# Row-wise argmax of an 8192 x 8192 matrix: loading row pairs as single 64 KB descriptors

## Chip, cores, metric

One core of one Trainium2 chip. The metric is the device time of one execution in microseconds (us), lower is better. Each kernel was executed several times, the kernel before always on the same chip in the same rounds. All runs quoted here are in the undisturbed (fast) state, with a granted TensorE clock of 1.0.

## The reference

```python
x = np.random.randn(8192, 8192).astype(np.float32)
def reference(x):
    return np.argmax(x, axis=1)
```

268 MB are read once; 8192 indices (64 KB) are written.

## The kernel before

The rows are worked on in 64 tiles of 128 rows (one row per partition, 32 KB). VectorE reduces a tile to the maxima of 128 chunks of 64 values (`cm`) and then to the row's maximum (`mx`). GpSimd copies the winning chunk of each row together (`ga`), ScalarE compares it with the maximum, TensorE sorts the matches into `sums`, and VectorE reads the place within the chunk out of them. The gathered copy is the last reader of a tile's 32 KB buffer, and it is put off (`defer`) until half of the next tile has been reduced, so that VectorE needn't wait for the small operations before it.

```python
xpool = ctx.enter_context(tc.tile_pool(name="x_sbuf", bufs=5))      # five buffers of 32 KB
# ...
def load_reduce(t, cm, loads, widths):
    xt = xpool.tile([P, M], F32, tag="xt")
    at = 0
    for w in loads:
        keep(nc.sync.dma_start(out=xt[:, at:at + w], in_=x[t * P:(t + 1) * P, at:at + w]))
        at += w
    at = 0
    for w in widths:
        # cm[:, chunks of this piece] = max over each chunk of 64
        keep(nc.vector.reduce_max(out=cm[:, c0:c1], in_=xt[:, at:at + w].rearrange(...), axis=AX.X))
        at += w
        step[0] = t * 8 + at // 1024
        run_due()                          # what was put off to this step
    return xt

def lookup(t, cm, xt, sums, k_after, last):
    # mx (VectorE), sc (ScalarE), wc (GpSimd) ...
    def copy_chunks():
        keep(nc.vector.reduce_max(out=k, in_=wc, axis=AX.X))
        # idx on GpSimd ...
        keep(nc.gpsimd.indirect_copy(ga, xt.rearrange("p (n h) -> p n h", h=H), idx, ...))   # frees xt
        # eq on ScalarE, 17 matmuls into sums ...
        if last:
            defer(12, lambda: finish(t - 3, 4, sums))
    defer(k_after, copy_chunks)

for t in range(63):
    # ...
    if t < 48:   loads, widths = [M], [M // 2] * 2        # whole tile in one transfer
    elif t < 60: loads = widths = [M // 2] * 2            # halves
    else:        loads = widths = [M // 4] * 4            # quarters
    xt = load_reduce(t, cm, loads, widths)
    lookup(t, cm, xt, sums, 4 if t < 60 else 2, t % 4 == 3)
# tile 63 has a direct way of its own ...
```

## Time and profile before

| | before |
|---|---|
| time, median | 642.61 us (642.29 to 643.03, 3 runs) |
| profiled span | 640.7 us |
| VectorE (DVE) busy | 596.8 us, 93% |
| DMA queue of x | 97.9% of 16 engines, 419 GB/s over the span |
| GpSimd, ScalarE, TensorE busy | 25%, 15%, 12% |

How to read it: the transfers of x are issued by SyncE (SP) on one queue, which 16 DMA engines work off. A buffer's next load can be issued when its last reader is done. As long as the queue never runs empty, the DMA engines set the pace; VectorE has about 0.4 us per tile to spare. The prediction below shows the lines.

### The profile page before, as it was taken

What the parts mean: (1) busy time and instruction counts of PE and PEld (TensorE: products, weight loads), DVE (VectorE), ACT (ScalarE), POOL (GpSimd) and SP (SyncE); (2) the same over time, 40 slices, a digit from 0 to 9 for tenths busy, and PEclk for the clock granted to TensorE, in tenths of its full rate; (3) what the DMA queues carried; (4) which work ended last, traced back from release to release, by engine and by line L of the source; (5) the groups of instructions that cost most, each with busy time, mean ns of one, the idle gap of its engine ahead of it and who ended that gap; (6) DMA issues with size and microseconds to landing.
All of it is one profiled execution on the core that took longest, in us unless ns stands there. A gap on an engine that the chain in (4) does not pass through costs nothing.

```text
span 640.7 us, 3237 instructions
## 1 busy us (share of the span) xinstructions
PE 77.0 (12%) x1079; PEld 66.7 (10%) x1079; DVE 596.8 (93%) x293; ACT 93.1 (15%) x130; POOL 160.0 (25%) x210
## 2 busy tenths in 40 slices
PE   0011010110110110110111101101101111110111
PEld 0011010110110110110110101101101110110110
DVE  1999989999999999999999999999999999999996
ACT  0011011011110110110110110111111110110121
POOL 4112212122122122222221221221221222222221
DMA  9999999999999999999999999999999999999991
GB/s 381 436 428 426 438 435 432 429 426 437 434 432 430 426 429 440 432 432 427 428 438 432 428 433 430 434 432 429 434 419 429 428 428 428 429 430 420 421 419 69
DMA packets 13233, 268.74 MB, mean 419 GB/s; under 512 B 1618, under 2 KB 1681, under 8 KB 2209
## 3 DMA queue, kind: packets, MB, share of 16 engines
q1 hardware_dynamic: 13104, 268.44, 97.9%
q8 instruction: 8, 0.13, 0.1%
q10 hardware_dynamic: 81, 0.06, 0.0%
q0 software_dynamic: 32, 0.03, 0.0%
q14 instruction: 8, 0.07, 0.0%
HBM read 268.47 MB, written 0.07 MB: 419 GB/s over the span
## 4 chain that ended last, share of the span: by engine, by line
issue 54%; POOL 21%; ACT 9%; DVE 8%; DMA 7%; POOLq 0%; PE 0%; ACTq 0%; SPq 0%; DVEq 0%
POOL ga L158 14%; DMA xt<-in_x_dram 7%; DVE cm L122 7%; ACT eq L160 5%; POOL wc L148 4%; ACT sc L147 3%; POOL idx L154 3%; DVE zi L221 0%; DVE z L217 0%; POOLq L158 0%; DVE k_all L152 0%; DVE mx L143 0%; PE ps L133 0%; ACTq L138 0%; DVE k_all L175 0%
## 5 line engine op out<-in xcount | busy, mean ns | idle before, releaser
L122 DVE TENSOR_REDUCE cm<-xt 128x64 f32<-128x4096 f32 (+2 forms) x137 | 564.4, 4126 | 33.4 <-DMA xt<-in_x_dram 32.3
L160 ACT ACTIVATE eq<-ga,mx 128x1024 bf16<-128x1024 f32 x63 | 72.3, 1148 | 512.6 <-POOL ga L158 512.6
L158 POOL INDIRECT_COPY ga<-xt,idx 128x1024 f32 x63 | 104.3, 1656 | 134.3 <-issue 130.0
L165 PEld LDWEIGHTS <-sel_flat 128*128 128x128 bf16 x1008 | 59.8, 127 | 546.4 <-issue 543.5
L165 PE MATMUL sums<-eq,sel_flat 128*128 128x64 bf16 x1008 | 63.8, 239 | 431.4 <-ACT eq L160 431.4
L154 POOL TENSOR_SCALAR idx<-starts,k_all 128x2 uint16<-128x2 f32 x63 | 19.2, 304 | 218.7 <-DVE k_all L152 217.2
L148 POOL TENSOR_TENSOR wc<-descC,sc 128x128 f32<-128x128 f32 x63 | 28.8, 457 | 117.0 <-ACT sc L147 117.0
L163 PE MATMUL sums<-descL,ones 1*128 1x64 bf16 x63 | 13.9, 224 | 117.8 <-DVE k_all L175 111.2
L147 ACT ACTIVATE sc<-cm,mx 128x128 f32<-128x128 f32 x63 | 24.4, 387 | 22.5 <-DVE mx L143 21.8
L143 DVE TENSOR_REDUCE mx<-cm 128x1 f32<-128x128 f32 x63 | 17.9, 284 | 4.8
L152 DVE TENSOR_REDUCE k_all<-wc 128x1 f32<-128x128 f32 x63 | 17.4, 276 | 0.4 <-POOL wc L148 0.4
L163 PEld LDWEIGHTS <-ones 1*128 1x128 bf16 x63 | 6.2, 98 | 12.0 <-POOL ones L87 6.4
L175 DVE TENSOR_REDUCE k_all<-sums 128x4 f32<-128x256 f32 (+1 forms) x16 | 6.6, 410 | 0.0
L132 PE MATMUL ps<-ident_m,k_all 128*60 128x128 f32 (+1 forms) x4 | 1.3, 420 | 5.9 <-DVE k_all L152 5.9
L188 POOL DMA_INDIRECT ga<-in_x_dram,idx x1 | 1.2, 1208 | 2.6 <-DVE idx L186 2.6
L81 POOL MEMSET sel_flat<- 128x2064 bf16 x1 | 1.8, 1818 | 0.0
L133 PE MATMUL ps<-ident,k_all 128*60 128x128 f32 (+1 forms) x4 | 1.3, 420 | 1.8 <-DVE k_all L175 1.8
L147 ACT ACT_TABLE_LOAD x1 | 1.3, 1283 | 0.7 <-PEq L252 0.7
L136 ACT ACTIVATE o<-ps 60x128 int32<-60x128 f32 (+1 forms) x2 | 0.6, 276 | 5.5 <-PE ps L133 5.5
L217 DVE MAX8 z<-xt 128x8 f32<-128x1024 f32 x1 | 1.2, 1221 | 0.0
L221 DVE FIND_INDEX8 zi<-z,xt 128x8 uint32<-128x1024 f32 x1 | 1.2, 1219 | 0.0
L82 POOL TENSOR_SCALAR sel_flat<-ident 128x128 bf16<-128x128 f32 x1 | 1.1, 1071 | 0.0
(32 smaller groups left out, 7.7 us busy)
## 6 DMA issues: line engine op xcount, KB each, us to landing
xt<-in_x_dram SPq DMA_DIRECT2D x48, 4096.0 KB, 29.9
xt<-in_x_dram SPq DMA_DIRECT2D x24, 2048.0 KB, 29.6
xt<-in_x_dram SPq DMA_DIRECT2D x14, 1024.0 KB, 21.1
xt<-in_x_dram SPq DMA_DIRECT2D x4, 512.0 KB, 14.5
out_dram<-o ACTq DMA_DIRECT2D x1, 60.0 KB, 6.1
ga<-in_x_dram,idx POOLq DMA_INDIRECT x1, 2.7
out_dram<-o ACTq DMA_DIRECT2D x1, 3.0 KB
out_dram<-o_last SPq DMA_DIRECT2D x1, 1.0 KB, 3.9
```

The lines of the kernel that those rows point to most:

```text
L81: nc.gpsimd.memset(sel_flat, 0.0)
L122: keep(nc.vector.reduce_max(out=cm[:, c0:c1], in_=xt[:, at:at + w].rearrange("p (c l) -> p c l", l=L), axis=AX.X))
L143: keep(nc.vector.reduce_max(out=mx, in_=cm, axis=AX.X))
L147: keep(nc.scalar.activation(out=sc, in_=cm, func=ACTF.Sign, bias=mx, scale=-1.0))
L148: keep(nc.gpsimd.tensor_tensor(out=wc, in0=descC, in1=sc, op=ALU.subtract))
L152: keep(nc.vector.reduce_max(out=k, in_=wc, axis=AX.X))
L154: keep(nc.gpsimd.tensor_scalar(out=idx, in0=starts, scalar1=k, scalar2=float(M), op0=ALU.subtract, op1=ALU.mult))
L158: keep(nc.gpsimd.indirect_copy(ga, xt.rearrange("p (n h) -> p n h", h=H), idx, i_know_this_is_slow=True))
L160: keep(nc.scalar.activation(out=eq, in_=ga, func=ACTF.Sign, bias=mx, scale=-1.0))
L163: nc.tensor.matmul(g, lhsT=ones, rhs=descL, start=True, stop=False)
L165: nc.tensor.matmul(g.rearrange("p (h l) -> p h l", h=2), lhsT=sel[:, r, :], rhs=eq.rearrange("p (h r) l -> p h r l", h=2)[:, :, r, :], sta ...
L175: keep(nc.vector.reduce_max(out=k2_all[:, t0:t0 + n], in_=sums[:, 0:n, :], axis=AX.X))
```

## The change

The intent: fewer and larger descriptors (a descriptor is one contiguous piece of a transfer, which the trace records as one packet). Rows 2p and 2p + 1 are neighbours in memory, so one descriptor of 64 KB brings both to partition p. Each five tiles come as pair, pair, single; a pair has a double buffer, so five buffers of 32 KB become two of 64 KB and one of 32 KB. Besides, tiles 48 to 53 come whole, the pieces of tiles 60 to 62 decrease, and the results of the paired rows have a store of their own.

```diff
-    xpool = ctx.enter_context(tc.tile_pool(name="x_sbuf", bufs=5))
+    xpool = ctx.enter_context(tc.tile_pool(name="x_sbuf", bufs=1))
 ...
-        xt = xpool.tile([P, M], F32, tag="xt")
+        if t % 5 in (0, 2):
+            xd = xpool.tile([P, 2, M], F32, tag="xd", bufs=2)
+            double[0] = xd
+            if t < PAIRED:                                     # PAIRED = 35
+                keep(nc.sync.dma_start(
+                    out=xd.rearrange("p j m -> p (j m)"),
+                    in_=x[t * P:(t + 2) * P, :].rearrange("(p j) m -> p (j m)", j=2)))
+        if t % 5 == 4:
+            xt = xpool.tile([P, M], F32, tag="xs", bufs=1)
+        else:
+            xt = double[0][:, (t % 5) % 2, :]
         at = 0
-        for w in loads:
+        for w in loads if t >= PAIRED or t % 5 == 4 else []:
 ...
-                defer(12, lambda: finish(t - 3, 4, sums))
+                defer(15, lambda: finish(t - 3, 4, sums))
 ...                          (store_paired: five small evictions and one store; cut)
-        if t < 48:
+        if t < 54:
             loads, widths = [M], [M // 2] * 2
 ...
-            loads = widths = [M // 4] * 4
+            loads = widths = [[4096, 2048, 2048], [3072, 3072, 2048], [3072, 2048, 2048, 1024]][t - 60]
```

Below, A and B are the two double buffers (tiles 0, 1 and 2, 3 of each five), S is the single one (tile 4).

More of the change, by code (lines that the diff above doesn't have):

```diff
@@ L35 @@
     NT = N // P
+    PAIRED = 35
     lpool = ctx.enter_context(tc.tile_pool(name="lead", bufs=1))
     gpool = ctx.enter_context(tc.tile_pool(name="gathered", bufs=2))
-    xpool = ctx.enter_context(tc.tile_pool(name="x_sbuf", bufs=5))
+    xpool = ctx.enter_context(tc.tile_pool(name="x_sbuf", bufs=1))
     epool = ctx.enter_context(tc.tile_pool(name="matches", bufs=2))
@@ L53 @@
     out_pairs = out_view([N, 2])
+    out_flat = out_view([2 * N])
     x_flat = x.tensor.reshape([N * C, L]).ap()
@@ L99 @@
     pending = []
+    double = [None]
     step = [0]
@@ L127, in load_reduce, with sum_parts, store_paired @@
         return xt
+    def sum_parts(ps, t0, n, step):
+        ts = slice(t0, t0 + (n - 1) * step + 1, step)
+        nc.tensor.matmul(ps, lhsT=k_all[:, ts], rhs=ident_m, start=True, stop=False)
+        nc.tensor.matmul(ps, lhsT=k2_all[:, ts], rhs=ident, start=False, stop=True)
+    def store_paired():
+        n = PAIRED // 5
+        o = opool.tile([n, 5 * P, 2], I32, tag="paired")
+        nc.gpsimd.memset(o, 0)
+        for u in range(5):
+            ps = ppool.tile([n, P], F32, tag="ps")
+            sum_parts(ps, u, n, 5)
+            if u < 4:
+                place = o[:, u // 2 * 2 * P:(u // 2 + 1) * 2 * P, 0].rearrange("c (p j) -> c p j", j=2)[:, :, u % 2]
+            else:
+                place = o[:, 4 * P:5 * P, 0]
+            keep(nc.scalar.activation(out=place, in_=ps, func=ACTF.Copy, scale=-1.0, bias=float(M + L)))
+        keep(nc.scalar.dma_start(out=out_flat[0:n * 10 * P].rearrange("(c q) -> c q", c=n),
+                                 in_=o.rearrange("c r two -> c (r two)")))
     def store(t0, n):
         ps = ppool.tile([n, P], F32, tag="ps")
-        nc.tensor.matmul(ps, lhsT=k_all[:, t0:t0 + n], rhs=ident_m, start=True, stop=False)
-        nc.tensor.matmul(ps, lhsT=k2_all[:, t0:t0 + n], rhs=ident, start=False, stop=True)
+        sum_parts(ps, t0, n, 1)
         o = opool.tile([n, P, 2], I32, tag=f"o{t0}")
@@ L175, in finish @@
         keep(nc.vector.reduce_max(out=k2_all[:, t0:t0 + n], in_=sums[:, 0:n, :], axis=AX.X))
+        if t0 == 4 * (PAIRED // 4):
+            store_paired()
         if t0 + n == 60:
-            store(0, 60)
+            store(PAIRED, 60 - PAIRED)
     def direct_begin(t, cm):
```

## The prediction

> **What bounds the kernel now.** I read the page first (engine shares, then the 40 slices), then the rates by stretch, then the waits, then the timeline of the first tiles, and last the chain of the final 90 us.
>
> ```profile
> DVE  1999989999999999999999999999999999999996
> DMA  9999999999999999999999999999999999999991
> L122 DVE TENSOR_REDUCE cm<-xt 128x64 f32<-128x4096 f32 (+2 forms) x137 | 564.4, 4126 | 33.4 <-DMA xt<-in_x_dram 32.3
> ```
>
> Two units look full. The DMA engines are busy in every slice but the last. VectorE is busy 93%, but the 33.4 us in which its reductions wait are nearly all put down to the load of x (13.1 us of them before the first tile). So the load of x sets the pace and VectorE follows closely: a tile costs DMA about 9.7 us and VectorE about 9.3 us (two reductions of 4.41 us, then mx and k_all, which add some 0.2 us each beyond overlap, and a quarter of the sums' 0.4 us).
>
> ```profile
> 100.00:200.00 100.00, 12.27 (x179) 10.90 (x179) 95.03 (x46) 15.85 (x22) 25.17 (x32) 1.00 1.00 430
> 480.00:590.00 110.00, 14.21 (x204) 12.58 (x204) 107.43 (x52) 17.29 (x24) 27.43 (x36) 1.00 1.01 427
> 592.00:612.00 20.00, 3.30 (x44) 2.65 (x44) 19.79 (x13) 4.03 (x5) 6.39 (x7) 1.00 1.01 421
> ```
>
> The last number of each line is GB/s, the one before it the DMA share. With descriptors of 32 KB (up to 479 us) it is about 431, with 16 KB 427, with 8 KB 421, always at full share. The engines never idle, so smaller descriptors cost time inside their own records. The packet records of the trace say how much: the median packet takes 161 ns at 4 KB, 312 at 8 KB, 614 at 16 KB and 1215 at 32 KB. Each doubling falls short of twice by 10, 10 and 13 ns, so a descriptor costs about 11 ns plus 36.7 ns per KB.
>
> ```profile
> 22.80 4.42 DVE L122 TENSOR_REDUCE cm<-xt 128x64 f32<-128x4096 f32 x1 [0.62 <-DMA xt<-in_x_dram]
> 27.14 0.28 DVE L152 TENSOR_REDUCE k_all<-wc 128x1 f32<-128x128 f32 x1
> 29.99 1.65 POOL L158 INDIRECT_COPY ga<-xt,idx 128x1024 f32 x1 [2.15 <-issue]
> 31.67 0.33 SPq L117 DMA_DIRECT2D xt<-in_x_dram  x1
> ```
>
> This is how a buffer comes free: tile 1 lands and its first half is reduced from 22.80; only then come tile 0's k, its index and its gathered copy; the copy ends at 31.64, and SP issues the load into tile 0's buffer at 31.67. That is **8.87 us from the landing of the next tile to the refill**. The refilled queue still holds 20 us of loads, so nothing is lost; the median of 29.9 us from issue to landing says the same (three tiles deep).
>
> ```profile
> 554.90 34.67 DMA xt<-in_x_dram
> 589.57 0.02 issue
> 589.60 4.43 DVE cm L122
> ```
>
> The chain leaves the load at 589.6 us; from there VectorE runs almost without a gap to the last result at 635.5. The end is the landing of tile 59's second half plus a fixed 46 us of VectorE and 5 us of final store.
>
> **What the Trainium skill says.** "DMA: Bandwidth & Descriptors", section "Where 436 GB/s comes from", puts the fabric ceiling at 435.2 GB/s; this trace, at 431, leaves under 1% to gain from any shape of descriptor. The same page under "Measured (HBM→SBUF, 128 partitions, SWDGE, issued from GpSimd)" gives about 10.5 ns per packet; my 11 ns from the packet records agrees, on loads issued from SP. Its section "Anatomy of one DMA — SWDGE (gpsimd) path" gives about 2.0 us of fixed cost per transfer, mostly completion. Here the first load is issued at 0.73 us and VectorE starts on it at 13.11: 12.4 us, of which 8 descriptors per engine are 9.7, so about 2.6 us on a cold queue. "VectorE: DVE Perf Modes", section "The perf-mode tier table (the rule you actually need)", has tensor_reduce at 1x only: 4096 values in 4414 ns agrees, and nothing in the change makes a reduction cheaper.
>
> **The change, part by part.**
> (a) 64 KB descriptors. Of 35 tiles, 28 go in 14 pairs. Each engine moves 8 descriptors per transfer, so 28 x 8 = 224 descriptors of 32 KB become 112 of 64 KB, if they are not cut up again. At 11 ns that saves 1.2 us. The 14 completions saved are about 9 ns each: 0.1 us. **Gain 1.3 us**, 0.2% of the span.
> (b) Tiles 48 to 53 in one transfer, not two: 6 x 8 descriptors fewer, **0.5 us**.
> (c) Tiles 60 to 62 have 10 pieces for 12: 16 descriptors fewer per engine, 0.2 us of DMA, and two reductions fewer. A reduction of 4096 takes 4414 ns and two of 2048 take 4552, so 0.14 us each: 0.3 us on VectorE's final run. The store of 60 rows, which now delays the 62nd tile's work (0.35 us wait of k_all on wc at 615.8), moves off. Together **0.6 us** on the path.
> (d) A pair lands as a whole and its buffer comes free as a whole. This is the cost. There are two double buffers (A, B) and a single one (S), filled A B S A B S. Pair A is free after its second tile's gathered copy, which happens in the middle of the first tile of B; that tile can start only when all of B has landed. So A's refill is issued 8.87 us after B's landing, and the only load left in the queue is S, which lands 9.72 us after B. Before, 20 us of loads were queued; now 0.85 us. A fresh transfer's first packet follows its issue by 1.0 us (first packet at 1.74 us in the trace, issue at 0.73), and data are gone from the queue some 0.34 us before the landing is seen. Bubble: 8.87 + 1.0 - (9.72 - 0.34) = **0.5 us at least**. To it comes what a dry queue pays at its start: the first packets of the run took 1.6 to 2.0 us, not 1.22, so 0.4 to 0.8 us. I take 0.35 to 0.65 of it, a bubble near 1.0 us. This happens at tiles 5, 10, 15, 20, 25, 30 and 35: **7 x 1.0 = 7 us**, between 3.4 and 10. B's refill is different: it is issued after tile 3's copy in the middle of tile 4, 18.6 + 8.87 = 27.5 us after B's landing, and A's data then last until about 29.7 us: just safe, by 1.2 us. S's refill is safe by 10 us. From tile 37 on, single loads land one by one and A's lead is 4 us and more again.
> (e) Something comes back: before, one of the 16 engines runs about 2.2 us behind the others by tile 16 (spread of the completion packets in the trace), and landings wait for it. In a bubble the others wait anyway and the lag goes away: **about 2 us** gained back.
> (f) VectorE starts at about 22.5 instead of 13.1 us. It waits for loads afterwards, so this is no loss by itself, but by tile 35 it is some 7 us behind the landings. At 9.72 - 9.28 = 0.44 us per tile it catches up in 16 tiles, by tile 51 to 55, before the tail at 59. Zero, but not by much. store_paired (five small evictions on ScalarE, one memset on GpSimd, a store) falls in an unpaired stretch on engines that are mostly idle: zero.
>
> Sum: 642.6 - 1.3 - 0.5 - 0.6 + 7 - 2 = 645.2; I shade it to **644.5**, since the cold-start term is the least certain one and a designer would hardly keep a change whose loss shows.
>
> **Rivals.** First, the gain with no bubble: if the refill reaches the queue in time (issue to first packet shorter than 1.0 us, or VectorE's half tile counted too long), it is 642.6 - 2.4 = 640.2. For it speaks that the margin in (d) is a few tenths; against it, that every term in (d) is read from this trace. Second, B's refills also come late: 1.2 us of margin is about one extra wait on GpSimd, and six or seven more bubbles make 649 to 652. Third, VectorE becomes the bound in the tail because it has not caught up: each tile missing costs 0.44 us, at most 2 to 3 us more. Fourth, 64 KB descriptors move data faster than the straight line says: the ceiling of 435 against 431 allows 1% of 273 us, 2.7 us, that is 638 at the very best with no bubble.
>
> **Range and chances.** The best combination is near 638, the central one 644.5, bubbles twice as costly 651. I take 640 to 649.5 for 8 in 10. A change of 2% needs 12.9 us either way: faster is beyond the fabric ceiling (1%), slower needs both A's and B's refills late and cold (3%).
>
> **What would show it.** Packets: 1792 data descriptors of 64 KB (14 x 128), some 2420 ns each, and 432 GB/s where the queue is full. Dips of the DMA share near 50, 100, 150, 200, 250, 300 and 350 us. VectorE's first reduction at about 22.5 us and its wait for x at some 45 to 50 us in all. In the timeline, the refill of A issued 8.9 us after the first reduction of a pair. Issue to landing of the pairs near 21 us for A. The tail chain from tile 59 to the end within 1 us of 51. I am wrong if the share shows no dips (then 640), if packets are still 32 KB (then only the bubbles remain), or if VectorE has no waits left in tiles 40 to 58 (then it has become the bound).

## The result and the profile after

| | before, same rounds | after |
|---|---|---|
| time, median of 5 runs | 642.29 us | 657.88 us (657.04 to 658.05) |
| ratio | | 1.0235, 95% interval 1.0221 to 1.0249 |

Ratios are the mean time of one kernel's fast runs over that of the other's of the same rounds, so not quite the ratio of the medians. The change is 2.3% slower, 15.6 us, and outside the predicted range.

From the page of the changed kernel: the busy tenths in 40 slices, and the group of the reductions (busy us, mean ns | idle before them and what ended it).

```profile
DVE  0699899899799899799799999999999999999997
DMA  9999999999999999998997999999999999999992
L137 DVE TENSOR_REDUCE cm<-xd 128x64 f32<-128x4096 f32 (+3 forms) x111 | 458.0, 4132 | 51.1 <-DMA xd<-in_x_dram 49.1
```

VectorE now shows an 8 or a 7 at every third slice (a slice is 16.4 us) through the first half of the run, and none after that until the last slice. It waits 49.1 us for x, not 32.3. The DMA row shows only two of the dips that were foreseen, as its 8 and its 7: an idle stretch of 1 to 2.5 us (below) is short beside a slice. The same stretch of five tiles in both kernels, in busy times by stretch (the last two numbers are the DMA share and GB/s); the first fence is the kernel after, from one landing of B to the next, the second the kernel before.

```profile
92.50:143.20 50.70, 5.88 (x89) 5.08 (x87) 46.17 (x21) 7.16 (x11) 12.04 (x15) 1.00 0.98 416
244.90:296.80 51.90, 6.03 (x86) 5.07 (x86) 46.50 (x22) 6.75 (x10) 12.05 (x15) 1.00 0.97 413
```

```profile
90.80:139.30 48.50, 5.90 (x85) 5.24 (x85) 45.44 (x20) 6.40 (x10) 11.57 (x15) 1.00 1.00 432
```

VectorE's work per five tiles is nearly the same (45.4 us before, 46.2 and 46.5 after); the cycle has become 2 to 3 us longer. (Each engine has its busy time and, in brackets, a count; VectorE's is the third pair.) Now the timeline of one refill of A in the changed kernel.

```profile
42.02 4.42 DVE L137 TENSOR_REDUCE cm<-xd 128x64 f32<-128x4096 f32 x1 [1.09 <-DMA xd<-in_x_dram]
46.35 0.28 DVE L186 TENSOR_REDUCE k_all<-wc 128x1 f32<-128x128 f32 x1
...
49.17 1.65 POOL L192 INDIRECT_COPY ga<-xd,idx 128x1024 f32 x1 [2.13 <-issue]
50.85 0.33 SPq L123 DMA_DIRECT2D xd<-in_x_dram  x1
...
72.72 4.42 DVE L137 TENSOR_REDUCE cm<-xd 128x64 f32<-128x4096 f32 x1 [2.97 <-DMA xd<-in_x_dram]
```

B lands and is started on at 42.02. Only after half of its first tile comes the gathered copy that frees A; the refill is issued at 50.85, **8.83 us** after the landing. It lands at 72.7, 21.9 us after its issue, while its eight descriptors per engine take 8 x 2.42 = 19.3 us. The remaining 2.5 us are the price of an empty queue. VectorE reaches the first tile of B at 42.02 and again, six rounds later, at 348.54: 51.1 us per five tiles, against 48.5 before. Tile 35 lands at 370.5 us and not at 354.5 (completions in the packet records plus the 0.34 us until VectorE sees them). So **16 us are lost in the first 35 tiles**, and the loss stays about the same to the end.

The packet records of the trace, which carry the start, length and size of every DMA packet, give the seven refills of A one by one. "Lead" is the mean time at which the 16 engines completed the previous transfer (each records a packet of 4 bytes then), less the issue of the refill. "Behind" is how much later the last engine completed B than the mean one. "Idle" is engine time with no packet, averaged over the 16 engines. "Slow" is what each engine's first two packets took beyond the usual 2418 ns each (1213 ns for tile 35's 32 KB), averaged in the same way.

| refill for tile | issued at | lead, us | B behind, us | idle, us | slow, us |
|---|---|---|---|---|---|
| 5 | 50.85 | 0.06 | 0.41 | 1.06 | 0.65 |
| 10 | 101.39 | -0.19 | 0.70 | 1.46 | 0.54 |
| 15 | 152.10 | -0.29 | 0.73 | 1.49 | 0.55 |
| 20 | 203.62 | -1.25 | 1.60 | 2.44 | 0.62 |
| 25 | 254.26 | -0.35 | 0.42 | 1.56 | 0.71 |
| 30 | 305.72 | -1.03 | 1.47 | 2.15 | 0.70 |
| 35 | 357.36 | -1.30 | 1.61 | 2.55 | 0.59 |
| sum | | | 6.9 | 12.7 | 4.4 |

Idle and slow add up to 17.1 us. There are 1792 packets of 64 KB with a median of 2418 ns, against two of 1213 ns: the fewer descriptors save 112 x 8 ns, 0.9 us. The balance, 16.2 us, agrees with the measured 16.0.

The end of the chain of work that ended last, in the changed kernel (start, length, what):

```profile
516.18 29.56 DMA xd<-in_x_dram
...
545.83 4.42 DVE cm L137
```

Before, the chain left the load at 589.6 us, at tile 59. Now it leaves it at 545.8, at tile 53, the last whole tile, and is on VectorE for the 106 us that follow, up to the final store.

### The profile page after: what moved, and what is told of

Its sections match the earlier page's. It is cut to its first block, busy times and chain, and to the rows that moved or that the text cites. A ratio compares the mean times of both kernels' runs of the same rounds, so it can differ in the third digit from the quotient of the medians.

```text
span 656.1 us, 3219 instructions
## 1 busy us (share of the span) xinstructions
PE 82.0 (12%) x1099; PEld 66.6 (10%) x1099; DVE 594.5 (91%) x291; ACT 94.6 (14%) x135; POOL 160.6 (24%) x211
## 4 chain that ended last, share of the span: by engine, by line
DVE 40%; DMA 29%; issue 19%; POOL 8%; ACT 3%; SPq 0%; DVEq 0%; POOLq 0%
DVE cm L137 38%; DMA xd<-in_x_dram 29%; POOL ga L192 6%; ACT eq L194 2%; POOL wc L182 1%; POOL idx L188 1%; ACT sc L181 1%; DVE k_all L186 1%; DVE mx L177 0%; DVE k_all L209 0%; DVE zi L258 0%; DVE z L254 0%; DVEq L177 0%; SPq L123 0%; DVE c L220 0%
## 5 line engine op out<-in xcount | busy, mean ns | idle before, releaser
L137 DVE TENSOR_REDUCE cm<-xd 128x64 f32<-128x4096 f32 (+3 forms) x111 | 458.0, 4132 | 51.1 <-DMA xd<-in_x_dram 49.1
L192 POOL INDIRECT_COPY ga<-xd,idx 128x1024 f32 x51 | 84.3, 1653 | 108.5 <-issue 108.5
L137 DVE TENSOR_REDUCE cm<-xt 128x64 f32<-128x4096 f32 x24 | 105.8, 4410 | 0.2 <-issue 0.2
L192 POOL INDIRECT_COPY ga<-xt,idx 128x1024 f32 x12 | 19.8, 1653 | 25.5 <-issue 25.5
L197 PE MATMUL sums<-descL,ones 1*128 1x64 bf16 x63 | 13.9, 224 | 53.1 <-DVE k_all L209 46.5
L147 PE MATMUL ps<-ident_m,k_all 128*7 128x128 f32 (+2 forms) x14 | 4.0, 406 | 10.7 <-DVE k_all L186 10.7
L148 PE MATMUL ps<-ident,k_all 128*7 128x128 f32 (+2 forms) x14 | 3.9, 409 | 6.5 <-DVE k_all L209 6.5
L161 ACT ACTIVATE o<-ps 7x128 int32<-7x128 f32 x5 | 1.7, 372 | 4.7 <-PE ps L148 4.6
## 6 DMA issues: line engine op xcount, KB each, us to landing
xd<-in_x_dram SPq DMA_DIRECT2D x16, 4096.0 KB, 19.4
xd<-in_x_dram SPq DMA_DIRECT2D x7, 1024.0 KB, 21.9
xd<-in_x_dram SPq DMA_DIRECT2D x5, 512.0 KB, 12.7
```

Source lines behind the costliest of these rows:

```text
L148: nc.tensor.matmul(ps, lhsT=k2_all[:, ts], rhs=ident, start=False, stop=True)
L197: nc.tensor.matmul(g, lhsT=ones, rhs=descL, start=True, stop=False)
```

## The experiments

The theory: a pair lands as a whole and frees its buffer as a whole, so A's refill comes when the queue has just run empty, and each such refill costs idle time and slow first packets. The rivals: 64 KB descriptors are slower by themselves; VectorE or the tail is what costs.

**e1: each pair in two transfers.** Buffers, rows, stores and tail as changed.

```diff
-                keep(nc.sync.dma_start(out=xd.rearrange("p j m -> p (j m)"), in_=...))
+                rows = x[t * P:(t + 2) * P, :].rearrange("(p j) m -> p j m", j=2)
+                for j in range(2):
+                    keep(nc.sync.dma_start(out=xd[:, j, :], in_=rows[:, j, :]))
```

> The changed kernel with each pair fetched in two transfers of 4 MB (even rows, then odd rows; 32 KB descriptors), buffers, rows, stores and tail as changed. Theory (dry queue: a pair lands as a whole, so the refill of A comes with 0.85 us of load left in the queue): tile 2 can start 9.7 us earlier relative to the end of its pair, the refill comes with 10 us still queued, no dips of the DMA share, about 642 us or a little less. Rival 1 (the double buffers or the strided rows or the store are what costs): still about 657. Rival 2 (64 KB descriptors are slower by themselves): about 642 too, so the next run must tell it from the theory.

Measured: 642.97 us (642.82 to 643.36), ratio 1.0008 (0.9991 to 1.0024). Its DMA row and its longest wait of VectorE for loads (us in total, times, longest):

```profile
DMA  9999999999999999999999999999999999999991
DVE cm L137 <- DMA xd<-in_x_dram: 28.2, 34, 12.8
```

The dips are gone, and 15 us with them. Double buffers, strided rows and the extra store cost nothing that shows. In the records, the refills that begin a pair found 8.5 to 10.0 us of transfer still queued; in the kernel before, refills found 18.1 to 19.4 us. So freeing a buffer only as a whole takes some 10 us of the lead, which costs nothing here; landing as a whole takes the rest, and that costs the time.

**e2 and e6: one transfer per pair, 32 KB descriptors.** In e2 the access pattern was only written in three dimensions.

```diff
-                    out=xd.rearrange("p j m -> p (j m)"),
-                    in_=x[t * P:(t + 2) * P, :].rearrange("(p j) m -> p (j m)", j=2)))
+                    out=xd,
+                    in_=x[t * P:(t + 2) * P, :].rearrange("(p j) m -> p j m", j=2)))   # e2
+                    in_=x[t * P:(t + 2) * P, :].rearrange("(j p) m -> p j m", j=2)))   # e6, stores adapted
```

> The changed kernel with each pair in one transfer, but the access pattern kept as 128 x 2 x 8192, which should give descriptors of 32 KB (the packet records must confirm it). Theory (dry queue): the seven dips stay, and 112 descriptors more per engine at 11 ns add 1.2 us: 658 to 660. Rival (64 KB descriptors are slower by themselves, mean record 2464 ns against 2 x 1219): about 642 to 645.

Measured in e2: 657.18 us (656.83 to 659.16), but its records still hold 1792 packets of 64 KB. The neighbouring rows had been joined all the same, so the run repeats the changed kernel and decides nothing. In e6 the two rows lie 4 MB apart.

> The run e2 was meant for this, but its descriptors were joined to 64 KB all the same. Here the pair is rows p and 128 + p of the two tiles, 32 KB each and apart in memory, in one transfer; the store places the results accordingly. Theory (landing as a whole is what costs): seven dips stay, and 112 descriptors more per engine at 11 ns add 1.2 us: 657.5 to 660. Rival (descriptors of 64 KB cost it): 642 to 645.

Measured in e6: 658.34 us (656.48 to 659.56), ratio 1.0243. No packet is over 32 KB (6912 have that size), and the records show idle stretches at the same seven refills, 11.9 us in sum. So the descriptors' size is cleared: **32 KB and 64 KB lose alike if the pair lands as one transfer, and e1 shows that it doesn't lose if it lands as two.**

**e7: the refill half a tile later.**

```diff
+        if t < PAIRED and t % 5 == 1:
+            k_after = 8                  # instead of 4: after all of the next tile
```

> The changed kernel with the gathered copy of pair A's second tile half a tile later (after 8192 instead of 4096 columns of the next tile): A's refill is issued 4.6 us later, seven times. Theory (refill on the critical path from B's landing to B's next landing): each cycle longer by the same 4.6 us, 657.9 + 7 x 4.6 = 690, range 687 to 693. Rival (VectorE's own work or the tail sets the end, the dips are mostly hidden): under 670.

Measured: 686.72 us in two runs, 28.8 us more than the changed kernel, 4.1 us for each of the seven refills. The first was issued at 55.14 instead of 50.85, 4.3 us later. Its DMA row:

```profile
DMA  9987997996996997899799599999999999999992
```

The way from B's landing to A's refill is on the critical path nearly one for one. The sum came 3 us short of the 690 expected; that the issue moved by 4.3 us and not by 4.6 explains 2 us of it.

**e8 and e14: the kernel before with three and with four buffers.**

```diff
-    xpool = ctx.enter_context(tc.tile_pool(name="x_sbuf", bufs=5))
+    xpool = ctx.enter_context(tc.tile_pool(name="x_sbuf", bufs=3))      # e8;  bufs=4 in e14
```

> The kernel before with three single buffers instead of five and nothing else: the refill is issued 8.87 us after the next landing and one load is left in the queue, the same lead of 0.85 us as pair A has in the changed kernel, but at every tile and with 32 KB descriptors. Theory (dry queue, independent of pairs): a loss at every tile, 0.5 us of idle engines and 0.65 us of slow first packets at most, so 0.5 to 1.2 us for each of some 58 tiles, 670 to 710, DMA share clearly below 1. Rival (pairs are what costs): 643 to 648.

> The kernel before with four single buffers instead of five: two loads are queued when a refill is issued, the second of which lands 19.4 us after the landing that started the wait of 8.87 us, so a lead of about 10 us. Theory (a lead of 3 to 4 us is enough): 642.3 to 643, no dips. Rival (short leads cost gradually, far beyond 4 us): 645 or more.

Measured: 711.77 us with three buffers (two runs), 642.49 us with four (642.05 to 642.69), ratio 0.9996. The DMA rows of e8 and of e14:

```profile
DMA  9999899999999997999999899898998999999992
```

```profile
DMA  9999999999999999999999999999999999999991
```

Without any pair, a lead as short (0.6 us in the mean of the refills up to tile 47 of e8, between -2.7 and 1.9) loses (711.77 - 642.89) / 61 = 1.1 us at each of the 61 tiles that wait for a buffer. Its 32 KB packets take 1293 ns in the mean instead of 1219. With the 8.4 to 9.9 us that e14's refills found queued, nothing is lost. So the fifth buffer of the kernel before was not needed for time, and pairs as such are not needed for the loss.

**e3 and e5: refills earlier.** In e3 A's copy comes at once after the maximum of its second tile, B's after 2048 columns of the next tile. In e5 both come after 1024 columns:

```diff
+        if t < PAIRED and t % 5 in (2, 4):
+            widths = [M // 8, 7 * M // 8]
+        k_after = 4 if t < 60 else 2
+        if t < PAIRED and t % 5 in (1, 3):
+            k_after = 1
```

> The changed kernel with both refills issued earlier: the gathered copy of a pair's second tile at once after its maximum for pair A (VectorE is waiting for the load then anyway), and after 2048 instead of 4096 columns of the next tile for pair B. Theory (dry queue): A is reissued some 4.4 us earlier, no dips, 64 KB descriptors at 432 GB/s, 640 to 643 us. Rival (64 KB descriptors slower by themselves): 650 or more, with packets of 64 KB still above 2440 ns in the mean. Rival (VectorE has become the bound): 652 or more, with no DMA dips and no waits of VectorE.

> The changed kernel with the gathered copy of each pair's second tile after 1024 instead of 4096 columns of the next tile (that tile reduced as 1024 + 7168, so no reduction more and no wait of VectorE for the small operations before it). A is reissued 5.65 us after B's landing, some 3.7 us before S has been moved, B some 4.4 us before A has been moved. Theory (a refill must be issued about 3 us before the queue's end, or its first packets are slow; if the queue runs dry, idle time comes on top): no dips, nearly no 64 KB packet above 2600 ns after the start, 641 to 642, the 1.3 us of fewer descriptors being the whole gain of pairs. Rival (64 KB transfers slow each other at every change of transfer, whatever the lead): 645 to 648 as in the run before, with slow packets at every refill.

Measured: e3 647.57 us (645.59 to 649.90), ratio 1.0089; e5 646.48 us (644.95 to 647.77), ratio 1.0058. From the page of e5 its DMA row, and from its timeline three refills of A:

```profile
DMA  9999999999999999999999999999999999999991
```

```profile
47.54 0.33 SPq L123 DMA_DIRECT2D xd<-in_x_dram  x1
...
145.78 0.33 SPq L123 DMA_DIRECT2D xd<-in_x_dram  x1
...
294.46 0.33 SPq L123 DMA_DIRECT2D xd<-in_x_dram  x1
```

The idle time is nearly gone (0.7 us over the seven refills of A, in e3 as in e5, instead of 12.7), and 10 to 11 us are won back, but neither expectation was met: against the kernel before, 5.0 us (e3) and 3.6 us (e5) stay. The records of e5 show what is left. The engines completed the transfer before these three refills at 50.91, 147.91 and 295.78 us in the mean, so the leads are 3.4, 2.1 and 1.3 us. Each engine's first two packets after the first of these refills were normal; after the second and third they were slow by 0.43 and 0.52 us together, in the mean of the engines. The leads shrink as one engine falls behind (the first and the last completion of B lie 0.5 us apart in the first round and 2.6 us in the fourth): the landing waits for it while the other fifteen eat up the queue.

The 21 refills of A in e3, e5 and e10 (below) together: the six with leads of 3.34 to 3.90 us cost at most 0.05 us each; the fifteen with 1.3 to 3.3 us cost from 0.12 to 0.78 us; at 0.1 us and less, in the changed kernel and e9, it is 0.54 to 0.80 us plus idle time. The two ends are clear. In between the lead alone doesn't order them, and B's refills in the changed kernel, at 2.4 to 2.8 us, cost under 0.1 us (first packets). Why these differ, and what makes the first packets slow, is open.

**e9, e10, e11: fewer matmuls.** The engine that falls behind does so where the records show a packet of 16 KB on a queue of kind "instruction", about every 70 us, at 96 and 166 us for instance; beside the one at 96 us a packet of x takes 1720 ns instead of 1213, and the spread of the completions grows from 0.95 to 1.65 us. To see whether that matters, 14 of the 16 selecting matmuls were left out for the first 40 tiles.

```diff
-            for r in range(R):
+            for r in range(R) if t >= 40 else (0, R - 1):
```

> The changed kernel with 2 instead of 16 selecting matmuls for each of the first 40 tiles; the result is wrong on purpose (the place within a chunk of those rows). It takes most of TensorE's instructions away, and with them the 16 KB instruction fetches that one DMA engine serves about every 70 us and that put that engine 1.0 to 1.3 us behind the others. Theory (a thin queue makes all engines wait for the one that was held up, where a deep queue hides it): the four or five fetches in the paired stretch fall to one or none, the spread of the completions stays near 0.6 to 1.2 us, idle time in the dips falls from 12.7 us in the sum to some 8, and the time by 3 to 5 us: 653 to 655. Rival (fetches don't matter): 657 to 658.

> The same cut of matmuls (wrong on purpose) in the version with early refills. Theory: with no engine held up the refills keep their lead of about 3 us, no slow packets after the start, 641 to 643 against 646.5 with all matmuls. Rival (pairs cost something else, fetches don't matter): 645 to 648.

> The same cut of matmuls (wrong on purpose) in the kernel before, as the control. Theory: 20 us of queued loads hide the held-up engine but for the last 2 us of spread, so 641 to 642.7. If it gains 4 us or more, the matmuls themselves cost something and the two runs before this say nothing of fetches.

Measured: 655.61 us for the changed kernel (657.88 with all matmuls), 644.86 us for e5's version (646.48), 641.70 us for the kernel before (642.89 in the same rounds). All three are wrong in half of the rows, as intended. The 16 KB packets fell from eight to four per run, so they do carry TensorE's instructions, and in the paired stretch of e9 only one at 327 us is left. The idle time of the seven refills fell from 12.7 to 10.0 us. But the control won 1.2 us as well, so only some 1 us at most is the fetches' special cost where the queue is thin (0.4 us by e10), which is hardly beyond the noise and less than the 3 to 5 us that I expected, and e10 missed its 641 to 643. The held-up engine is a part of the loss, not its core.

**e4 and e12: the tail alone**, on the kernel before, without pairs. Both have the decreasing pieces and the later maximum of the sums; e4 also has whole tiles up to 53.

```diff
-        if t < 48:
+        if t < 54:                                             # e4 only
-            loads = widths = [M // 4] * 4
+            loads = widths = [[4096, 2048, 2048], [3072, 3072, 2048], [3072, 2048, 2048, 1024]][t - 60]
-                defer(12, lambda: finish(t - 3, 4, sums))
+                defer(15, lambda: finish(t - 3, 4, sums))
```

> The kernel before with only the other parts: whole transfers up to tile 53, the uneven pieces of tiles 60 to 62, and the sums' maximum three steps later; no pairs, five single buffers. As predicted these gain 1.1 us: 641.5. Against it: after a whole-tile landing VectorE is 4.8 us behind once halves begin, and six tiles of halves at 0.5 us each win back only 3 us of it, so it would enter the tail about 1.5 us late: 643 to 644.

> The kernel before with the uneven pieces of tiles 60 to 62 and the later maximum of the sums, but halves from tile 48 as before. If the later change to halves was what ate the tail's gain (VectorE enters the tail about 1.5 us late), this is 641.5 to 642.2, 0.5 to 1 us under the kernel before. If the uneven pieces bring nothing, 642.6.

Measured: e4 642.81 us (642.70 to 643.15), ratio 1.0005 (0.9988 to 1.0022); e12 642.00 us (641.91 to 642.49), ratio 0.9989 (0.9975 to 1.0003). The last load in the chain of e4, then of e12:

```profile
499.60 30.92 DMA xt<-in_x_dram
```

```profile
564.65 30.25 DMA xt<-in_x_dram
594.99 4.42 DVE cm L122
```

With whole tiles up to 53, the chain leaves the load at 530.5 us and VectorE is behind from there on; with halves from tile 48 it leaves it at 595.0. The reading of this: a whole-tile landing puts VectorE about half a tile (4.6 us) behind the halves that follow, and six tiles of halves are too few to win that back. In the medians the pieces gain what part (c) said or a little more, and part (b) takes it away; but both intervals include no difference, so of these sizes only the place where VectorE falls behind is shown. e12 is the fastest correct version here, by 0.9 us in the medians of these rounds.

**e13 and e15: one pair in five.** One double and three single buffers, in the order pair, single, single, single, with e12's tail. e15 also has the pair's copy after 1024 columns.

```diff
-        if t % 5 in (0, 2):
-            xd = xpool.tile([P, 2, M], F32, tag="xd", bufs=2)
+        if t % 5 == 0:
+            xd = xpool.tile([P, 2, M], F32, tag="xd", bufs=1)
-        if t % 5 == 4:
-            xt = xpool.tile([P, M], F32, tag="xs", bufs=1)
+        if t % 5 >= 2:
+            xt = xpool.tile([P, M], F32, tag="xs", bufs=3)
```

> Two in five of the first 35 tiles as one pair (64 KB descriptors) and three in five alone, one double and three single buffers, order pair, single, single, single; tail as in e12. Whenever a refill is issued, about 10 us of loads or more are queued: the pair's refill comes 8.87 us after the landing of the first single with two singles behind it, and a single's refill finds at least a pair or two singles. Theory (lead alone): no dips and no slow packets after the start; 7 pairs save 56 descriptors per engine at 11 ns, 0.6 us, against e12: 641.0 to 641.8. Rival (64 KB transfers or double buffers cost something at any lead): 643 or more.

> e13 with the gathered copy of the pair's second tile after 1024 instead of 4096 columns of the next tile: each of the seven refills of the pair is issued 3.2 us earlier, so its lead goes from 1.5 down to -0.8 in e13 to 4.7 down to 2.4, the low end where one engine lags. Theory (lead alone): no dips, few slow packets, 641.5 to 643 (e12 less 0.6 us at best). Rival (64 KB transfers cost something at any lead): 645 or more.

Measured: e13 650.13 us (648.74 to 651.23), ratio 1.0110; e15 643.20 us (642.21 to 644.13), ratio 1.0011 (0.9997 to 1.0025). My expectation of e13 was wrong in its working, which the timeline of e13 shows:

```profile
90.31 4.41 DVE L137 TENSOR_REDUCE cm<-xt 128x64 f32<-128x4096 f32 x1
...
99.11 0.33 SPq L123 DMA_DIRECT2D xd<-in_x_dram  x1
```

The first single had landed at 81.1 us, but VectorE, which had just been handed two tiles at once, got to it only at 90.31. The refill at 99.11 therefore met a queue with 0.7 us left, not 10. So a pair shortens the lead twice: its buffer comes free late, and it makes VectorE late. With 3.2 us more (e15) there is almost no idle time, but five of the seven refills after pairs, at leads of 2.1 to 3.3 us, still have slow packets, 0.10 to 0.49 us each; the other two, at 3.5 and 4.0 us, have none. No version reached leads over 3.4 us at all of its refills, so the 0.6 to 1.3 us that fewer descriptors should bring were never seen in a time; they are seen only in the packets' medians.

## Why the prediction was wrong

**Part (a), the descriptors,** was right in kind: 1792 packets of 64 KB, 2418 ns each (2420 foreseen). The saving is 8 ns per descriptor rather than 11. (The 36.7 ns per KB beside it holds for KB of 1000 bytes; with 1024, as everywhere else here, it is 37.6.)

**Part (d) named the right mechanism and mis-sized its term.** The places (tiles 5 to 35), the 8.87 us from B's landing to the refill (8.83 measured) and the safety of B's refill all held, and e1, e6, e7 and e8 confirm the mechanism. The term "7 x 1.0 = 7 us" measured 17.1 us. Two of its parts failed.

- "Bubble: 8.87 + 1.0 - (9.72 - 0.34) = 0.5 us at least" lets all 16 engines finish together with the landing that VectorE sees. A landing is that of the last engine, and the others are done with B 0.4 to 1.6 us earlier (6.9 us over the seven refills in the table). They run out of S earlier by as much. The lead was to be 9.38 - 8.87 = 0.5 us; it was 0.06 to -1.30. This is the larger part of the 10 us. (Some 2 us more: the engines' first packets came 1.2 us after the issue in the mean, not 1.0, and small differences of the spacing.) The spread stood in the packet records of the kernel before, and I used it for another step.
- "I take 0.35 to 0.65 of it": the slow start measured 0.54 to 0.71 us per refill, the upper end each time. I had also read the start of the run too low: its 16 first packets took 1.61 to 2.39 us, 0.68 us over the usual 1.215 in the mean. And my 1.0 us was the sum of 0.5 and a middle value, without a spread.

**Part (e) failed too.** I added 2 us for a lag that the bubbles would absorb. Where the queue is deep, the lag costs once: from tile 15 to 57 of the kernel before it stays at 2.2 to 2.3 us. In the bubbles it does go away, but not for good: S's completions were 2.15 us apart before the refill for tile 20, those of that refill 0.66 us, and 1.95 us again two transfers later, after the fetch packet at 249 us. And while it lasts, it makes the next bubble longer, which is the column "B behind". At tile 35 the completions were still 1.7 us apart, so at most half a us came back.

**Parts (b) and (c)** were to gain 1.1 us together. e12 agrees with (c) in its median (0.9 us), and e4 with (b) taking it back, since VectorE enters the tail behind; neither is clear of the noise. That is the third rival in a small size and by another cause: it had caught up with the loads by tile 53 (it waits 0.4 us there), and fell behind at the change from whole tiles to halves.

**Part (f)** held: VectorE's first reduction started at 22.70 us, it reached tile 35 at 376.6 us, 6 us after the landing (some 7 foreseen), and it caught up by tile 50 (51 to 55 foreseen), where it waits for a load again (0.4 us). So pairing didn't leave it behind at tile 53. Its wait for x, foreseen at 45 to 50 us, was 49.1.

**The shading** by 0.7 us, because a designer would hardly keep a change whose loss shows, was no reading of the profile and pointed away from the result. The sum with the terms as measured or bounded here is 642.3 - 0.9 (a) + 17.1 (d) - 0.5 (e) = 658.0, with (b) and (c) at nothing; measured were 657.88.

## What to carry to other kernels

In a kernel that is bound by its loads, work out for each refill how much transfer is still queued when it can be issued, counted to the first engine to run dry and not to the landing that the consumer sees; here A's refills wanted some 3.4 us, and 8 to 10 us were ample. Merging two loads into one makes both landing and release coarser and takes the lead away at both ends (18 to 19 us became none here); a descriptor's 8 ns didn't pay for that. When piece sizes change along a kernel, see where the consumer is left behind at the change.

## What the Trainium skill lacked or had wrong

- "DMA: Bandwidth & Descriptors", section "Anatomy of one DMA — SWDGE (gpsimd) path", gives about 2.0 us of fixed cost per transfer, for transfers issued from GpSimd. What it lacks is when that cost shows. On the loads issued from SP here it depends on what is queued: with a full queue 32 KB loads complete 9.7 us apart, all of it packets; a pair that met an empty queue took 21.9 us from issue to use with 19.3 us of packets, so 2.5 us.
- No page that I read says how early a transfer must be issued to leave the engines unaffected. Here the first two packets of A's refills were 0.1 to 0.8 us slow at leads of 1.3 to 3.3 us, with little idle time (at most 0.3 us), and normal from about 3.4 us.
- "Runtime: NRT & Kernel Launch": its section "The ~15µs preamble/postamble breakdown" says that instructions are fetched over a port of their own, its section "Instruction fetch mechanics" that they come in blocks of 16 KiB by a DMA queue. This trace fits the second: it has "instruction" packets of 16 KB (about 1.0 us), halved in number when matmuls were left out. What the page lacks is that a fetch holds up a load: a packet of x beside one took 1720 ns instead of 1213.
- No page gives a figure for how far the engines of one queue drift apart: here their completions of one transfer lay 0.6 us apart at the start and 2.2 us apart for most of the kernel before.
